# Twelve-tile down projections by single column groups, and a new order for the last down pairs, in a two-layer encoder on one core

## The chip, the core and the metric

The kernel runs on one core of a Trainium2 chip. Such a core has a matrix engine (PE, "TensorE"; its weight loads are shown apart as PEld), a vector engine (DVE), a scalar engine (ACT), GpSimd (POOL), and a sync engine (SP), which here issues the DMAs. Each engine works through its own instructions in the order in which they stand, and waits for the others by semaphores. The metric is the device time of one launch in microseconds (us); less is better. Before the change it was 2042.35 us (median of 3 runs, 2038.47 to 2043.43).

## What is computed

An encoder trunk of two layers over 256 tokens of 2048 features, all in float32: layer 0 mixes tokens by attention, layer 1 by a gated linear recurrence, and each is followed by the same feed-forward part:

```python
D_MODEL = 2048; SEQ = 256; DEPTH = 2
D_FF = -(-8 * D_MODEL // (3 * 256)) * 256        # 5632

def swiglu(h, w_gate, w_up, w_down):
    return (jax.nn.silu(h @ w_gate) * (h @ w_up)) @ w_down

def reference(x, ...):
    for i in range(DEPTH):
        h = rms_norm(x, norm_mix[i])
        mix = attention_mixer(...) if i % N_MIXERS == 0 else recurrent_mixer(...)
        x = x + mix
        x = x + swiglu(rms_norm(x, norm_ffn[i]), w_gate[i], w_up[i], w_down[i])
    return x
```

The change lies in the feed-forward part alone.

## The kernel before

**Numbers in two parts.** A float32 value is held as a high part `hi` (a cast to the matmul's format) and a low part `lo` (the value less `hi`). A product of two tiles is three matmuls: high by high, high by low, low by high. Weights come from memory as blocks `raw` of 512 KB: two tiles of 128 input features, each by 512 output columns (`load_half`, L109). ACT casts a block to `hi` (L122), DVE subtracts to get `lo` (L123). There are five buffers of each of `raw`, `hi` and `lo`, so the cast of a block waits until PE has finished the block five before it. Token tiles are the stationary side of a matmul, weights the moving one, and results gather in accumulators `acc` of 128 tokens by 512 columns. There are four of these (`ps_a`); four more (`pm`) hold other sums.

**The feed-forward part** (`ffn`, L760). The 5632 hidden features are 44 tiles, worked through in three parts of 12, 16 and 16 (`PARTS`). In each part, units of four hidden tiles are made from all 16 tiles of the normalized input (`unit`, L761): one column group of the gate weights and one of the up weights. Then silu, scalings, and a turn from token rows to feature rows (`turned`, L444: two DVE transposes `tb`, then sixteen small ACT copies `tf`), after which ACT writes each hidden tile's high part (`act`, L775) and DVE its low part (L776). When the units of a part are done, `down` (L493) multiplies the part's hidden tiles by its share of the down weights and adds the result to the residual `x_tok`. The output has four column groups of 512.

**Pairs and seven products.** `project_pair` (L276) takes two column groups together (gate and up, or two groups of the down weights) and two halves of the tokens, so it fills all four accumulators. It goes through pairs of input tiles in steps. An ordinary step reads two weight blocks, one for each column group, and makes four products from each. Two steps of each call are made in another way: seven products on sums of blocks instead of eight products. For these, `seven_forms` (L245) makes sums of two weight blocks on DVE (`wx`, L252 to L255), their high part on ACT (`wxh`, L259) and low part on DVE (`wxl`, L260), and `x_forms` (L264) sums of the token tiles. Five of the seven results go through separate sums in `pm`, which `merge` (L317) combines on DVE; `down` then adds them to the residual (L500), apart from the accumulators' own adds (L509). `SEVEN` gives the two steps that are so made, by the number of steps, and `USUAL_STEPS` and `FIRST_STEPS` the order of the steps. A down of 12 tiles has six steps a call, 0, 2, 1, 4, 3, 5, of which 1 and 3 are of seven products.

**One column group at a time.** `output` (L476) and `project_tokens` (L223), which serve the attention's and the recurrence's output projections, take one column group after the other with two accumulators each, all in plain products.

**What sets the order.** PE's order is the order of the code. The other engines' orders, SP's DMA queue among them, are set at build time by a scheduler that goes by the order in which the code asks for things and by its own reckoning of times; on the chip nothing overtakes. `half` (L162) hands out the weight blocks in the order of a list, `order`, and `ffn_order` (L137) builds the feed-forward part of that list, so the steps' order must be the same there and in `project_pair`. The last down of the first layer also feeds the next normalization: `norm.add` (L410) squares a finished column group (`nj`), turns it, and writes the operands `xg` (L404, L405) of the recurrent layer. The last down of the second layer sends each finished group to memory.

## Time and profile before

| | |
|---|---|
| median of 3 runs | 2042.35 us |
| the profiled execution, its device time | 2042.2 us |
| its span, first to last instruction | 2040.4 us |
| mean granted PE clock | 0.990 |
| PE, DVE, ACT busy | 98%, 84%, 65% of the span |
| memory read | 382.13 MB |

The page gives shares of the whole span. In its groups of instructions, a line such as "L282 PE MATMUL acc<-hi,act" names the source line, the engine, the operation and the tiles: out of a weight block's high part and a hidden tile into an accumulator. The view of waits gives, for an engine, the line that waited, the line it waited for, the time in all, how often, and the longest. The windows give busy times and the granted clock for stretches of the span. The view in order of time has a start, a duration and, in brackets, the idle time before an instruction and what ended it. Successive matmuls overlap, so their pace is read from their starts.

### The profile page before, as it was taken

Reading aid. Unit: us, or ns where it says so; the run is one execution under the profiler, and the core shown is the slowest. Engines: PE = TensorE matmul, PEld = TensorE weight load, DVE = VectorE, ACT = ScalarE, POOL = GpSimd, SP = SyncE. Lnnn points to the kernel's source line nnn. Section 1 sums busy time; section 2 is a strip of 40 time slices with the busy share of each in tenths; the row PEclk is TensorE's granted clock in tenths of the full one; section 3 lists DMA queues with packets and bytes.
Section 4 is the critical chain, followed back from the end, with each engine's and each line's share of the span. In section 5 each row is a group of like instructions: output and inputs, shape, how many; then the busy total and the mean of one; then the engine's idle time right before and its main releaser. Section 6 shows DMA issues by size and latency. Waiting matters only on the chain.

```text
span 2040.4 us, 27933 instructions
## 1 busy us (share of the span) xinstructions
PE 1999.7 (98%) x9920; PEld 1691.3 (83%) x9920; DVE 1721.6 (84%) x2447; ACT 1336.3 (65%) x2070; POOL 166.6 (8%) x213
## 2 busy tenths in 40 slices
PE   9999999989999999999899999999989999999999
PEld 8898888867888888888799998888768888888887
DVE  7998789877888878889868877889787889878987
ACT  7665767654667546676689987767535766457663
POOL 1563000000000000000133330000000000000000
PEclk9999999989999999999899999999999999999999
DMA  8444565555556665555646555555545566555664
GB/s 318 156 135 146 184 209 194 186 172 189 186 184 198 208 213 186 186 190 193 200 157 197 180 167 186 186 196 196 177 168 180 188 197 225 190 193 186 204 218 145
DMA packets 109004, 386.06 MB, mean 189 GB/s; under 512 B 12224, under 2 KB 12992, under 8 KB 108736
## 3 DMA queue, kind: packets, MB, share of 16 engines
q1 hardware_dynamic: 108720, 384.26, 56.9%
q8 instruction: 78, 1.28, 0.2%
q14 instruction: 62, 0.51, 0.1%
q10 hardware_dynamic: 144, 0.02, 0.0%
HBM read 382.13 MB, written 2.10 MB: 188 GB/s over the span
## 4 chain that ended last, share of the span: by engine, by line
PE 69%; DVE 17%; DMA 6%; issue 5%; ACT 3%; SPq 0%; POOL 0%; DVEq 0%; ACTq 0%
PE acc L282 38%; PE acc L235 8%; DVE lo L123 7%; PE pm L282 5%; PE acc L213 5%; DMA raw<-in_w_up_dram 4%; PE acc L328 3%; PE acc L327 3%; PE acc L329 3%; ACT tf L456 1%; DMA raw<-in_w_down_dram 1%; ACT hi L122 1%; PE pm L328 1%; PE pm L329 1%; PE pm L327 1%
## 5 line engine op out<-in xcount | busy, mean ns | idle before, releaser
L122 ACT CAST hi<-raw 128x1024 fp32r<-128x1024 f32 (+1 forms) x708 | 730.5, 1047 | 510.9 <-PE acc L282 384.7
L123 DVE TENSOR_TENSOR lo<-raw,hi 128x1024 fp32r<-128x1024 f32 (+1 forms) x708 | 855.0, 1226 | 133.4 <-ACT hi L122 129.6
L282 PE MATMUL acc<-hi,xg 128*128 128x512 f32 x2200 | 698.2, 390 | 9.8 <-DVE x_tok L509 6.0
L282 PEld LDWEIGHTS acc<-hi,xg 128*128 128x128 f32 x2200 | 413.4, 188 | 103.2 <-issue 7.8
L282 PE MATMUL acc<-lo,xg 128*128 128x512 f32 x1100 | 428.6, 390 | 0.0
L282 PE MATMUL acc<-hi,act 128*128 128x512 f32 x1072 | 349.7, 399 | 14.9 <-ACT act L775 7.5
L282 PEld LDWEIGHTS acc<-hi,act 128*128 128x128 f32 x1072 | 205.5, 192 | 65.9 <-ACT act L775 8.3
L282 PEld LDWEIGHTS acc<-lo,xg 128*128 128x128 f32 x1100 | 206.8, 188 | 42.4
L282 PE MATMUL acc<-lo,act 128*128 128x512 f32 x536 | 212.1, 396 | 0.0
L456 ACT COPY tf<-tb 32x256 f32<-32x256 f32 x448 | 181.2, 404 | 8.4 <-DVE xg L405 1.2
L235 PE MATMUL acc<-hi,act 128*128 128x512 f32 x512 | 159.8, 390 | 0.0
L327 PE MATMUL acc<-xg,hi 128*128 128x256 f32 x512 | 146.8, 287 | 3.5 <-ACT xg L404 3.4
L252 DVE TENSOR_TENSOR wx<-raw,raw 128x512 f32<-128x512 f32 x68 | 47.1, 692 | 120.0 <-DMA raw<-in_w_up_dram 89.3
L328 PE MATMUL acc<-xg,hi 128*128 128x256 f32 x512 | 146.5, 286 | 0.8 <-DVE xg L405 0.7
L329 PE MATMUL acc<-xg,lo 128*128 128x256 f32 x512 | 145.9, 285 | 0.0
L260 DVE TENSOR_TENSOR wxl<-wx,wxh 128x1536 fp32r<-128x1536 f32 x68 | 119.2, 1753 | 15.1 <-ACT wxh L259 14.8
L259 ACT CAST wxh<-wx 128x1536 fp32r<-128x1536 f32 x68 | 100.6, 1479 | 44.2 <-DVE wx L255 40.3
L213 PE MATMUL acc<-xg,hi 128*128 128x512 f32 x384 | 126.1, 396 | 0.1
L282 PEld LDWEIGHTS acc<-lo,act 128*128 128x128 f32 x536 | 103.1, 192 | 21.2
L235 PEld LDWEIGHTS acc<-hi,act 128*128 128x128 f32 x512 | 96.1, 188 | 19.6
L327 PEld LDWEIGHTS acc<-xg,hi 128*128 128x128 f32 x512 | 99.7, 195 | 3.9 <-ACT xg L404 3.9
L328 PEld LDWEIGHTS acc<-xg,hi 128*128 128x128 f32 x512 | 99.6, 195 | 1.3 <-DVE xg L405 1.3
(239 smaller groups left out, 2846.3 us busy)
## 6 DMA issues: line engine op xcount, KB each, us to landing
raw<-in_w_gate_dram SPq DMA_DIRECT2D x176, 512.0 KB, 4.4
raw<-in_w_up_dram SPq DMA_DIRECT2D x176, 512.0 KB, 4.2
raw<-in_w_down_dram SPq DMA_DIRECT2D x176, 512.0 KB, 4.3
raw<-in_w_in_dram SPq DMA_DIRECT2D x64, 512.0 KB, 4.4
raw<-in_w_qv_dram SPq DMA_DIRECT2D x40, 512.0 KB, 4.3
raw<-in_w_o_dram SPq DMA_DIRECT2D x32, 512.0 KB, 3.5
raw<-in_w_out_dram SPq DMA_DIRECT2D x32, 512.0 KB, 3.8
graw<-in_w_gates_dram SPq DMA_DIRECT2D x32, 256.0 KB, 3.5
```

The lines of the kernel that those rows point to most:

```text
L122: newest["cast"] = act.copy(hi[:, sl, :], raw[:, sl, :])
L123: dve.tensor_tensor(lo[:, sl, :], raw[:, sl, :], hi[:, sl, :].bitcast(F32), ALU.subtract)
L213: pe.matmul(o, w, x, start=(k == 0 and not part), stop=(k == total - 1 and not part))
L235: pe.matmul(accs[a], x, wt[:, k, :], start=(k0 + k == 0 and n == 0), stop=(end and k == 1 and n == 2))
L252: dve.tensor_tensor(x[:, 0, :], r2[:, 0, :], r1[:, 0, :], ALU.add)
L259: act.copy(xh, x)
L260: dve.tensor_tensor(xl, x, xh[:].bitcast(F32), ALU.subtract)
L282: pe.matmul(acc, a, b, start=id(acc) not in begun, stop=last and i == 2)
L327: pe.matmul(o, hi, x[:, :S], start=start, stop=False)
L328: pe.matmul(o, hi, x[:, S:], start=False, stop=False)
L329: pe.matmul(o, lo, x[:, :S], start=False, stop=stop)
L456: act.copy(o, y)
```

## The change

Downs of 12 tiles no longer use seven-product steps. They go through `output`: four column groups, one after the other, each through steps 0 to 5 in order with two accumulators, and their residual adds are those of `output`. No token sums are made for that part. Downs of 16 tiles stay as they were, apart from the last part's: there each pair of column groups runs its steps together up to and with the second seven-product step (step 5), and then steps 6 and 7 for the first column group and after that for the second. The second pair of the last part also takes step 3 before step 2. `project_pair` now hands each column group's accumulators to a function `done` as soon as they are finished. The list of weight blocks follows.

```diff
-SEVEN = {6: (1, 3), 8: (2, 5)}
-USUAL_STEPS = {6: (0, 2, 1, 4, 3, 5), 8: (0, 1, 2, 3, 4, 5, 6, 7)}
+SEVEN = (2, 5)
+USUAL_STEPS = (0, 1, 2, 3, 4, 5, 6, 7)
 FIRST_STEPS = (0, 1, 3, 4, 2, 6, 5, 7)
+LAST_STEPS = (0, 1, 3, 2, 4, 5, 6, 7)
...
+    def pair_plan(steps, apart):
+        m = 1 + steps.index(SEVEN[-1]) if apart else len(steps)
+        return [(n, (0, 1)) for n in steps[:m]] + [(n, (j,)) for j in range(2) for n in steps[m:]]
+
+    def unit_steps(first):
+        return FIRST_STEPS if first else USUAL_STEPS, False
+
+    def down_steps(p, second):
+        last = p == len(PARTS) - 1
+        return LAST_STEPS if second and last else USUAL_STEPS, last
...
             down = wide(f"w_down{l}_{p}")
+            if n != KT:
+                seq += down
+                continue
             for c in range(0, len(down), n):
-                for k in pair_steps(n // 2):
-                    seq += [down[c + k], down[c + n // 2 + k]]
+                for k, cols in pair_plan(*down_steps(p, c > 0)):
+                    seq += [down[c + n // 2 * j + k] for j in cols]
...
-    def project_pair(xs, forms, middle, first=False):
+    def project_pair(xs, forms, order, middle, done):
...
-        steps = pair_steps(len(xs) // 2, first)
-        seven = [n for n in steps if n in forms]
-        for n in steps:
+        steps = pair_plan(*order)
+        seven = [n for n in order[0] if n in forms]
+        for n, cols in steps:
...
-                for j in range(2):
+                for j in cols:
                     half()
                     hi, lo = (flat(t) for t in newest["tiles"])
+                    end = n == order[0][-1]
                     for a in range(2):
                         for k in range(2):
-                            product(banks[j][a], tokens(2 * n + k, a), (hi[:, k, :], lo[:, k, :]), n == steps[-1] and k == 1)
-        return banks
+                            product(banks[j][a], tokens(2 * n + k, a), (hi[:, k, :], lo[:, k, :]), end and k == 1)
+                    if end:
+                        done(j, banks[j])
...
-            banks = project_pair(xs, forms, middle)
-            for j in range(2):
+            def done(j, accs):
                 for a in range(2):
...
-                        dve.tensor_tensor(y, y, banks[j][a][:, sl], ALU.add)
+                        dve.tensor_tensor(y, y, accs[a][:, sl], ALU.add)
...
+            project_pair(xs, forms, down_steps(p, c > 0), middle, done)
...
-            for i, n in enumerate(seven):
-                if first <= 2 * n < len(hid):
+            for i, n in enumerate(SEVEN):
+                if forms is not None and first <= 2 * n < len(hid):
                     forms[n] = x_forms(hid[2 * n], hid[2 * n + 1], f"hf{i}")

         for p, n in enumerate(PARTS):
-            hid, forms = [], {}
+            hid, forms = [], {} if n == KT else None
...
-            down(hid, forms, nxt if last else None, last and nxt is None)
+            if n == KT:
+                down(hid, forms, p, nxt if last else None, last and nxt is None)
+            else:
+                output(hid)
```

In `unit`, the adds, silu and scalings that stood after `project_pair` move into a `done` of its own, for each column group as it ends.

How the order of instructions moves on the engines is shown at three places. First DVE, at the end of the third unit of the first layer's twelve-tile part: from the adds of the up accumulators (`fu<-acc`) to the transposes. Before:

```order
L123 TENSOR_TENSOR lo_4424<-raw_4422,hi_4423 128x1024
L769 TENSOR_TENSOR fu_4246<-acc_4011,fu_4246 128x512
L769 TENSOR_TENSOR fu_4246<-acc_4012,fu_4246 128x512
L260 TENSOR_TENSOR wxl_4448<-wx_4446,wxh_4447 128x1536
L770 SCALAR_TENSOR_TENSOR fu_4246<-fu_4246,nr_3271,fg_4245 128x512 x2
L123 TENSOR_TENSOR lo_4442<-raw_4440,hi_4441 128x1024
L123 TENSOR_TENSOR lo_4451<-raw_4449,hi_4450 128x1024
L448 STREAM_TRANSPOSE tb_4332<-fu_4246 128x512 x2
```

After:

```order
L124 TENSOR_TENSOR lo_4402<-raw_4400,hi_4401 128x1024
L786 TENSOR_TENSOR fu_4226<-acc_3991,fu_4226 128x512
L786 TENSOR_TENSOR fu_4226<-acc_3992,fu_4226 128x512
L787 SCALAR_TENSOR_TENSOR fu_4226<-fu_4226,nr_3271,fg_4225 128x512 x2
L124 TENSOR_TENSOR lo_4420<-raw_4418,hi_4419 128x1024
L462 STREAM_TRANSPOSE tb_4312<-fu_4226 128x512 x2
```

The block sums' low part and one of two weight rows ahead of the transposes are gone.

Second ACT, a little later at the same place: the sixteen copies and the casts that write the hidden tiles' high parts (`act`). Before:

```order
L456 COPY tf_4333<-tb_4332 32x2x128 x16
L122 CAST hi_4523<-raw_4522 128x1024
L122 CAST hi_4532<-raw_4531 128x1024
L122 CAST hi_4576<-raw_4575 128x1024
L775 CAST act_4352<-tf_4333 128x256
```

After:

```order
L470 COPY tf_4313<-tb_4312 32x2x128 x16
L123 CAST hi_4459<-raw_4458 128x1024
L123 CAST hi_4477<-raw_4476 128x1024
L795 CAST act_4332<-tf_4313 128x256
L795 CAST act_4335<-tf_4313 128x256
```

Two weight casts stand between the copies and the hidden tiles, where there were three. The two belong to the first two blocks of the second column group.

Third DVE again, where that down ends and the next unit begins: the residual adds that free the last accumulators. Before:

```order
L123 TENSOR_TENSOR lo_4926<-raw_4924,hi_4925 128x1024
L254 TENSOR_TENSOR wx_4948<-raw_4951,raw_4942 128x512
L500 TENSOR_TENSOR x_tok<-x_tok,fg_4815 128x512
L500 TENSOR_TENSOR x_tok<-x_tok,fu_4816 128x512
L509 TENSOR_TENSOR x_tok<-x_tok,acc_4617 128x512
L123 TENSOR_TENSOR lo_4944<-raw_4942,hi_4943 128x1024
L255 TENSOR_TENSOR wx_4948<-wx_4948,raw_4942 128x512
L509 TENSOR_TENSOR x_tok<-x_tok,acc_4616 128x512
L509 TENSOR_TENSOR x_tok<-x_tok,acc_4618 128x512
```

After:

```order
L264 TENSOR_TENSOR wx_4874<-raw_4877,raw_4868 128x512
L265 TENSOR_TENSOR raw_4877<-raw_4877 128x512
L124 TENSOR_TENSOR lo_4834<-raw_4832,hi_4833 128x1024
L266 TENSOR_TENSOR wx_4874<-raw_4877,raw_4868 128x512
L267 TENSOR_TENSOR wx_4874<-wx_4874,raw_4868 128x512
L124 TENSOR_TENSOR lo_4852<-raw_4850,hi_4851 128x1024
L498 TENSOR_TENSOR x_tok<-x_tok,acc_4680 128x512
L498 TENSOR_TENSOR x_tok<-x_tok,acc_4681 128x512
```

The merged sums' adds are gone. All four block-sum operations of the next unit's first seven-product step stand ahead of the last two residual adds.

More of the change, by code (lines that the diff above doesn't have):

```diff
@@ L132, in wide @@
         return [(src[c, i], HALF) for c in range(src.shape[0]) for i in range(src.shape[1])]
-    def pair_steps(n, first=False):
-        return FIRST_STEPS if first else USUAL_STEPS[n]
+    def pair_plan(steps, apart):
[6 more added lines that the diff above has]
+        return LAST_STEPS if second and last else USUAL_STEPS, last
     def ffn_order(l):
@@ L141, in ffn_order @@
             for _ in range(n // FOUR):
-                for k in pair_steps(KT // 2, i == 0):
-                    seq += [u[i + k] for u in units]
+                for k, cols in pair_plan(*unit_steps(i == 0)):
+                    seq += [units[j][i + k] for j in cols]
                 i += KT // 2
             down = wide(f"w_down{l}_{p}")
+            if n != KT:
+                seq += down
+                continue
             for c in range(0, len(down), n):
-                for k in pair_steps(n // 2):
-                    seq += [down[c + k], down[c + n // 2 + k]]
+                for k, cols in pair_plan(*down_steps(p, c > 0)):
+                    seq += [down[c + n // 2 * j + k] for j in cols]
         return seq
@@ L414, in add @@
                 self.operand(f, True)
-            for n in SEVEN[KT // 2] if self.seven else ():
+            for n in SEVEN if self.seven else ():
                 if FOUR * c <= 2 * n < FOUR * c + FOUR:
@@ L490, in output, with down @@
             norm.finish()
-    def down(xs, forms, norm=None, end=False):
+    def down(xs, forms, p, norm=None, end=False):
         for c in (0, 2):
@@ L760, in ffn, with unit, done @@
     def ffn(norm, nxt):
-        def unit(hid, forms, seven, first):
+        def unit(hid, forms, first):
             got = []
-            banks = project_pair(norm.xs, norm.forms, lambda *banks: got.extend(merge(*banks)), first)
-            g, u = got
-            for a, acc in enumerate(banks[0]):
-                dve.tensor_tensor(g[:, a, :], acc, g[:, a, :], ALU.add)
-                table_act(g[:, a, :], g[:, a, :], AF.Silu, scale=norm.rt[:, a : a + 1])
-            for a, acc in enumerate(banks[1]):
-                dve.tensor_tensor(u[:, a, :], acc, u[:, a, :], ALU.add)
-                dve.scalar_tensor_tensor(u[:, a, :], u[:, a, :], norm.rt[:, a : a + 1], g[:, a, :], ALU.mult, ALU.mult)
+            def done(j, accs):
+                g, u = got
+                for a, acc in enumerate(accs):
+                    if j == 0:
+                        dve.tensor_tensor(g[:, a, :], acc, g[:, a, :], ALU.add)
+                        table_act(g[:, a, :], g[:, a, :], AF.Silu, scale=norm.rt[:, a : a + 1])
+                    else:
+                        dve.tensor_tensor(u[:, a, :], acc, u[:, a, :], ALU.add)
+                        dve.scalar_tensor_tensor(u[:, a, :], u[:, a, :], norm.rt[:, a : a + 1], g[:, a, :], ALU.mult, ALU.mult)
+            project_pair(norm.xs, norm.forms, unit_steps(first), lambda *banks: got.extend(merge(*banks)), done)
+            u = got[1]
             first = len(hid)
@@ L777, in unit @@
                 hid.append(h)
-            for i, n in enumerate(seven):
-                if first <= 2 * n < len(hid):
+            for i, n in enumerate(SEVEN):
+                if forms is not None and first <= 2 * n < len(hid):
                     forms[n] = x_forms(hid[2 * n], hid[2 * n + 1], f"hf{i}")
         for p, n in enumerate(PARTS):
-            hid, forms = [], {}
+            hid, forms = [], {} if n == KT else None
             for i in range(n // FOUR):
-                unit(hid, forms, SEVEN[n // 2], p == i == 0)
+                unit(hid, forms, p == i == 0)
             last = p == len(PARTS) - 1
@@ L788, in ffn @@
                 ln_exp_tables()
-            down(hid, forms, nxt if last else None, last and nxt is None)
+            if n == KT:
+                down(hid, forms, p, nxt if last else None, last and nxt is None)
+            else:
+                output(hid)
     nr = Norm("norm_mix", KT)
```

## The prediction

> **What bounds the kernel now.** I read the page first, then who waits for whom on TensorE (PE), then the windows with the granted clock, and last the order in time round both twelve-tile down projections.

> ```profile
> span 2040.4 us, 27933 instructions
> PE 1999.7 (98%) x9920; PEld 1691.3 (83%) x9920; DVE 1721.6 (84%) x2447; ACT 1336.3 (65%) x2070; POOL 166.6 (8%) x213
> ...
> PE acc L282 <- DVE x_tok L509: 11.1, 7, 2.4
> PE acc L282 <- ACT act L775: 7.5, 2, 3.8
> PE acc L282 <- DVE fg L766: 4.5, 10, 0.9
> PE acc L327 <- ACT xg L404: 3.4, 1, 3.4
> ...
> PE pm L282 <- DVE wxl L260: 1.4, 1, 1.4
> ```

> PE sets the time; all it lost is in such waits and in slow stretches after them. The waits name the places: residual adds that free an accumulator (L509) and hidden tiles that are late (L775) are 18.6 of them. The next rows are windows (us, each engine's busy time and count, granted clock, DMA share, GB/s): both down projections with their edges, then three stretches inside the first.

> ```profile
> core 0: us, PE busy (x) PEld busy (x) DVE busy (x) ACT busy (x) POOL busy (x), PEclk, DMA share, GB/s
> 394.90:476.70 81.80, 71.82 (x290) 56.30 (x289) 68.25 (x83) 42.02 (x54) 0.00 (x0) 0.94 0.52 170
> 1445.00:1529.00 84.00, 73.72 (x291) 57.64 (x289) 68.30 (x83) 41.49 (x54) 0.00 (x0) 0.91 0.49 164
> ...
> 411.60:422.60 11.00, 6.80 (x17) 4.80 (x17) 6.51 (x8) 6.87 (x11) 0.00 (x0) 0.69 0.43 153
> 436.00:443.00 7.00, 4.68 (x14) 3.13 (x13) 6.66 (x10) 2.43 (x3) 0.00 (x0) 0.76 0.44 137
> 471.00:478.00 7.00, 3.82 (x16) 2.54 (x16) 7.00 (x10) 2.60 (x3) 0.00 (x0) 1.00 0.37 107
> ```

> Now PE in order of time: start, duration, instruction, and in brackets the idle time before it and what ended that.

> ```profile
> 394.94 0.39 PE L282 MATMUL acc<-hi,xg 128*128 128x512 f32 x1
> ...
> 406.58 0.39 PE L282 MATMUL acc<-hi,act 128*128 128x512 f32 x1
> ...
> 411.34 0.39 PE L282 MATMUL acc<-wxh,act 128*128 128x512 f32 x1
> 415.49 0.80 PE L282 MATMUL acc<-hi,act 128*128 128x512 f32 x1 [3.76 <-ACT act L775]
> ...
> 438.59 0.50 PE L282 MATMUL acc<-hi,act 128*128 128x512 f32 x1 [2.32 <-DVE x_tok L509]
> ...
> 470.38 0.39 PE L282 MATMUL acc<-hi,xg 128*128 128x512 f32 x1
> ...
> 474.30 0.50 PE L282 MATMUL acc<-hi,xg 128*128 128x512 f32 x1 [2.40 <-DVE x_tok L509]
> ...
> 476.73 0.47 PE L282 MATMUL acc<-hi,xg 128*128 128x512 f32 x1 [0.78 <-DVE x_tok L509]
> ...
> 1445.08 0.39 PE L282 MATMUL acc<-hi,xg 128*128 128x512 f32 x1
> ...
> 1529.20 0.77 PE L282 MATMUL acc<-hi,xg 128*128 128x512 f32 x1 [0.44 <-DVE x_tok L509]
> ```

> Matmuls overlap, so a duration of 0.39 is not their price. The 21 matmuls of a seven-product step start between 406.58 and 411.34: 4.76 / 21 = **0.2267 us each**; a product of three is 0.68, a weight block of four products 2.72. From 394.94 (the unit's last matmul) to 476.73 (the 13th of the next unit) PE issues 1 + 276 + 12 = 289. At full pace that is 65.5; it took 81.79, so 16.3 are lost: the three waits, the slow stretches, and some 0.7 at the unit's end, where the fg adds behind block sums free the first accumulators late. In the second layer (1445.08 to 1529.20) it took 84.12: 18.6 lost. These 34.9 are the prize.

> **The change, part by part.**

> *Extra matmuls.* A twelve-tile down has 92 products now (two pairs of column groups, each four steps of eight products and two of seven) and 96 after. Four products of three, two layers: 24 x 0.2267 = **+5.4**. Nothing hides them.

> *The first wait: hidden tiles of the last unit.* DVE and ACT in time:

> ```profile
> 397.73 1.28 DVE L769 TENSOR_TENSOR fu<-acc,fu 128x512 f32<-128x512 f32 x2
> 398.93 1.75 DVE L260 TENSOR_TENSOR wxl<-wx,wxh 128x1536 fp32r<-128x1536 f32 x1
> 400.59 1.41 DVE L770 SCALAR_TENSOR_TENSOR fu<-fu,nr,fg 128x512 f32<-128x512 f32 x2
> 401.92 2.36 DVE L123 TENSOR_TENSOR lo<-raw,hi 128x1024 fp32r<-128x1024 f32 x2
> 404.19 1.30 DVE L448 STREAM_TRANSPOSE tb<-fu 128x512 f32<-128x512 f32 x2
> ...
> 405.52 6.65 ACT L456 COPY tf<-tb 32x256 f32<-32x256 f32 x16
> 412.19 2.94 ACT L122 CAST hi<-raw 128x1024 fp32r<-128x1024 f32 x3
> 415.04 1.32 ACT L775 CAST act<-tf 128x256 fp32r<-128x256 f32 x4
> ...
> 416.68 1.43 DVE L776 TENSOR_TENSOR act<-tf,act 128x256 fp32r<-128x256 f32 x4
> ```

> Let T be the unit's end on PE, 394.94 + 0.23 = 395.2. The transposes end at T+10.3, the copies at T+17.0, and PE goes on at T+20.3 although it got there by T+16.4. After the change this chain loses the block sums: behind the two fu adds stand the two scalings, one weight row and the transposes, so about 0.2 + 1.28 + 1.41 + 1.18 + 1.30 = T+5.4. Sixteen copies: T+12.0. Two weight casts instead of three, 2 x 0.98: T+14.0; first tile's cast: T+14.3. But PE is there sooner too: it needs tile 8 after four weight blocks, 4 x 2.72 = T+10.9, since the order is now by column group. So the wait stays, about 3.4. The tile's low half stands behind the low halves of two weight blocks on DVE: about T+15.7, with the third matmul due at T+14.8: 0.9 more. Bounds: 0, if the chain outruns this, to 9.4, if operands still come at T+20.3. The queues' new order, not the old time, speaks for 4.3. Behind the casts ACT also holds weight casts, but those are for blocks that PE reaches later.

> Then the slow stretch. The window 411.60:422.60 has a mean clock of 0.69: (1 - 0.69) x 11.0 = 3.4 lost. I take 3.4 again. First wait after: 3.4 + 0.9 + 3.4 = **7.7 per layer**.

> [...]

> *The second and third wait: accumulators.* There are four accumulators. A pair of column groups takes all four, so the next pair (438.59) and the next unit (474.30, 476.73) wait until DVE has added them into x_tok, and DVE has merges and block sums in between:

> ```profile
> 466.42 0.69 DVE L252 TENSOR_TENSOR wx<-raw,raw 128x512 f32<-128x512 f32 x1 [0.25 <-DMA raw<-in_w_up_dram]
> ...
> 472.36 0.68 DVE L500 TENSOR_TENSOR x_tok<-x_tok,fg 128x512 f32<-128x512 f32 x1
> ...
> 473.56 0.68 DVE L509 TENSOR_TENSOR x_tok<-x_tok,acc 128x512 f32<-128x512 f32 x1
> ```

> After the change a column group takes two, and the other two have a whole group, 6 x 2.72 = 16.3, to be added: hidden. At the next unit, its first block uses the accumulators of the group before the last; the last group's are needed 2.72 and 4.08 after the down's end. Before those adds DVE has the next unit's four block-sum operations and two weight rows. The first of them now runs at 466.42, 4.0 ahead of the next unit's start at 470.38; four at 0.60 a step and two at 1.14 end 0.7 after it, and the adds at 1.3 and 1.9. That is in time by 1.4. If the cover goes, PE waits one for one, up to today's 2.40 + 0.78 here. I take 0.

> Both spans then need 301 x 0.2267 = 68.2 plus 7.7 = 75.9: **-5.9** against 81.79, **-8.2** against 84.12; the extra matmuls are inside.

> *The last part's pairs.* The products are the same. In each pair the last two steps run one column group, then the other; the first group's accumulators are finished 5.44 before the pair's end, not 2.72, and their adds and normalization start earlier. In the second pair step 2 (seven products) follows step 3. Where the first layer's normalization lies over block sums, PE waits 1.4 for wxl; with step 2 later I take it as gone: **-1.4**, bounds -1.4 to +3 (the same wait, doubled, at step 2). Weight DMAs on SP move with the steps, and one output DMA of the second layer is put ahead of one more weight DMA; that block is used only in the fourth step, so PE's 16.3 of earlier products hide it. Exposed, it would cost a landing, under 5.

> After the first layer PE waits for the next normalization and for gate operands:

> ```profile
> 996.21 0.58 PE L327 MATMUL acc<-xg,hi 128*128 128x256 f32 x1 [3.45 <-ACT xg L404]
> 997.46 0.58 PE L328 MATMUL acc<-xg,hi 128*128 128x256 f32 x1 [0.66 <-DVE xg L405]
> ...
> 1014.53 0.35 PE L327 MATMUL pm<-xs,ghi 128*128 128x256 f32 x1 [1.44 <-DVE xs L364]
> ```

> The third column group's adds may start 2.7 earlier, but one more weight cast and weight row stand ahead of the same xg rows, and gate DMAs move ahead of weights. I take 0, between -4.1 (3.45 + 0.66 gone) and +3.4 (another slow stretch). At the kernel's end the last accumulator is the same one: 0.

> **Sum.** -5.9 - 8.2 - 1.4 = -15.5 on a span of 2040.4: 2024.9. The profiled execution took 2042.2, so 1.8 lie around its span, and the median of the runs is 2042.35: **2027 us**.

> **Rivals.**
> 1. *The first wait goes.* The chain is 6 us shorter, and ACT need only run a little earlier than I count. For: DVE is freed. Against: sixteen copies (6.65) alone fill most of T+10.9. 2027 - 2 x 7.7 = 2012.
> 2. *The next unit still waits.* The last group's adds stay behind block sums that wait for a DMA (0.25 at 466.42). Today's price is 2.40 + 0.78, with half of a 3.4 slow stretch about 4.9 per layer: 2037. Against: 1.4 of slack.
> 3. *No slow stretch* follows the first wait. For: not every wait has one, 2.40 at 474.30 had none (1.00 in 471:478). Against: 2.32 had one, and 3.76 one of 3.4. Without it in both layers: 2027 - 2 x 3.4 = 2020. [...]
> 4. *Slower: every column group waits for its accumulators.* If DVE falls behind by more than the 16.3 of a group, each of the four group ends per layer costs what one costs now: (2.32 + 2.40 + 0.78) / 2 and a slow stretch of (1 - 0.76) x 7.0 = 1.7 make 4.5. That is 8 x 4.5 = 36 put on 2027: 2063. For: DVE is 84% busy. Against: without block sums a group needs six weight rows (7.4) and two adds (1.4) of those 16.3.
> 5. *The wait only moves*: operands still at T+20.3, so 9.4 + 3.4 per layer: 2027 + 2 x 5.1 = 2037.

> **Numbers.** Forecast 0.68, rivals in order 0.07, 0.08, 0.08, 0.04, 0.05. The likeliest one's own range is 2020 to 2034, two slow stretches either way. For 8 in 10 I take 2015 to 2037: it leaves out rival 4, most of rival 1, and the forecast's tails. What can be told from no change is 0.3%, 6.1 us, so faster means below 2036.2: the forecast, rivals 1 and 3 and half of 2, some 0.87. Rival 5 and the rest of 2 make 0.08 for no change; rival 4 and a tail 0.05.

> **What would show it.** In the new profile: 24 more matmuls; no wait on a residual add of the down (x_tok) in either down or at the unit behind it; a wait of 3 to 4 for the act cast, some 11 us into each down, with a half-clock stretch behind it; no wait on wxl in the first layer's last part. Each span from unit's end to the 13th matmul of the next unit should be 73 to 79. Accumulator waits at column group ends, a first wait over 6 or none, or a new wait of more than 3 where the recurrent layer starts would each prove a step wrong.

## The result and the profile after

The changed kernel takes **2028.24 us** (median of 4 runs, 2026.79 to 2030.66) against 2041.95 for the kernel before (4 runs, the three named above and one more): a ratio of 0.9936, 95% interval 0.9919 to 0.9954. It is faster by 13.7 us. The forecast was 2027, with a range of 2015 to 2037. The profiled execution took 2027.33; its span is 14.9 shorter than the one before (2040.4).

The page of the changed kernel: the span, the engines' busy time, and then PE's first waits (what waited, for whom, us in all, times, longest).

```profile
span 2025.5 us, 27859 instructions
PE 1994.5 (98%) x9944; PEld 1690.0 (83%) x9944; DVE 1665.6 (82%) x2347; ACT 1318.7 (65%) x2054; POOL 167.4 (8%) x213
...
PE acc L294 <- DVE fg L783: 5.9, 9, 1.6
PE acc L247 <- ACT act L795: 5.3, 2, 2.7
PE pm L294 <- DVE wxl L272: 2.3, 1, 2.3
PE acc L341 <- ACT xg L418: 2.3, 1, 2.3
...
PE acc L342 <- DVE xg L419: 1.8, 1, 1.8
PE acc L247 <- DVE act L796: 1.5, 2, 0.7
...
PE acc L294 <- DVE x_tok L522: 0.6, 1, 0.6
```

PE has the 24 matmuls more, DVE 100 instructions and 56 us less. The 11.1 of waits on residual adds (x_tok) are down to 0.6, and that one stands in the last part. The wait for the hidden tiles (act) is there, once in each layer. The wait for wxl, forecast to go, grew from 1.4 to 2.3.

The two spans (from the start of the unit's last matmul to the start of the 13th of the next unit) as windows of the changed kernel, and then the stretch behind the first wait; the columns are those of the windows before.

```profile
394.77:468.61 73.84, 70.43 (x303) 57.51 (x301) 42.78 (x48) 35.21 (x46) 0.00 (x0) 0.98 0.56 177
1439.57:1513.39 73.82, 70.41 (x302) 57.50 (x301) 42.75 (x48) 35.21 (x46) 0.00 (x0) 0.98 0.55 178
408.70:415.10 6.40, 5.66 (x16) 4.18 (x17) 3.57 (x6) 2.64 (x5) 0.00 (x0) 0.73 0.68 229
```

DVE's work in a span fell from 68.3 to 42.8. PE's 301 matmuls ask 301 x 0.2267 = 68.24, so 5.6 are lost in each span, where 16.3 and 18.6 were. PE in order of time shows where they are in the first layer:

```profile
394.77 0.39 PE L294 MATMUL acc<-hi,xg 128*128 128x512 f32 x1
394.99 0.39 PE L247 MATMUL acc<-hi,act 128*128 128x512 f32 x1
...
405.65 0.39 PE L247 MATMUL acc<-hi,act 128*128 128x512 f32 x1
408.70 0.50 PE L247 MATMUL acc<-hi,act 128*128 128x512 f32 x1 [2.67 <-ACT act L795]
...
410.18 0.74 PE L247 MATMUL acc<-hi,act 128*128 128x512 f32 x2 [0.74 <-DVE act L796]
...
465.89 0.39 PE L294 MATMUL acc<-hi,xg 128*128 128x512 f32 x1
...
468.38 0.61 PE L294 MATMUL acc<-hi,xg 128*128 128x512 f32 x2
```

There is one wait of 2.67, one of 0.74 right behind it, a slowed stretch (a clock of 0.73 over 6.4: 1.7 lost), some 0.5 of starts and ends, and then nothing up to the next unit and in it.

### The profile page after: what moved, and what is told of

It is laid out like the page before. It is cut to its first block, busy times and chain, and to the rows that moved or that the text cites. A ratio compares the mean times of both kernels' runs of the same rounds, so it can differ in the third digit from the quotient of the medians.

```text
span 2025.5 us, 27859 instructions
## 1 busy us (share of the span) xinstructions
PE 1994.5 (98%) x9944; PEld 1690.0 (83%) x9944; DVE 1665.6 (82%) x2347; ACT 1318.7 (65%) x2054; POOL 167.4 (8%) x213
## 3 DMA queue, kind: packets, MB, share of 16 engines
q8 instruction: 78, 1.28, 0.3%
## 4 chain that ended last, share of the span: by engine, by line
PE 74%; DVE 14%; issue 4%; DMA 4%; ACT 3%; POOL 0%; SPq 0%; DVEq 0%; ACTq 0%; POOLq 0%
PE acc L294 38%; PE acc L247 14%; DVE lo L124 6%; PE pm L294 6%; PE acc L225 4%; DMA raw<-in_w_up_dram 3%; PE acc L342 3%; PE acc L341 3%; PE acc L343 3%; ACT tf L470 1%; PE pm L342 1%; PE pm L343 1%; PE pm L341 1%; ACT hi L123 1%; DVE tb L462 1%
## 5 line engine op out<-in xcount | busy, mean ns | idle before, releaser
L123 ACT CAST hi<-raw 128x1024 fp32r<-128x1024 f32 (+1 forms) x708 | 729.9, 1046 | 512.3 <-PE acc L294 331.3
L247 PE MATMUL acc<-hi,act 128*128 128x512 f32 x896 | 281.5, 393 | 6.8 <-ACT act L795 5.3
L294 PE MATMUL acc<-hi,act 128*128 128x512 f32 x800 | 253.7, 390 | 1.8 <-DVE fg L783 1.2
L247 PEld LDWEIGHTS acc<-hi,act 128*128 128x128 f32 x896 | 169.6, 189 | 43.5 <-ACT act L795 6.2
L294 PEld LDWEIGHTS acc<-hi,act 128*128 128x128 f32 x800 | 150.2, 188 | 36.2 <-issue 3.2
L247 PE MATMUL acc<-lo,act 128*128 128x512 f32 x448 | 175.6, 392 | 0.0
L294 PE MATMUL acc<-lo,act 128*128 128x512 f32 x400 | 155.7, 389 | 0.0
L264 DVE TENSOR_TENSOR wx<-raw,raw 128x512 f32<-128x512 f32 x60 | 41.5, 692 | 126.3 <-DMA raw<-in_w_up_dram 102.5
L272 DVE TENSOR_TENSOR wxl<-wx,wxh 128x1536 fp32r<-128x1536 f32 x60 | 105.0, 1751 | 11.2 <-ACT wxh L271 11.2
L271 ACT CAST wxh<-wx 128x1536 fp32r<-128x1536 f32 x60 | 88.7, 1478 | 38.4 <-DVE wx L267 35.5
```

The lines of the kernel that those rows point to most:

```text
L123: newest["cast"] = act.copy(hi[:, sl, :], raw[:, sl, :])
L247: pe.matmul(accs[a], x, wt[:, k, :], start=(k0 + k == 0 and n == 0), stop=(end and k == 1 and n == 2))
L264: dve.tensor_tensor(x[:, 0, :], r2[:, 0, :], r1[:, 0, :], ALU.add)
L271: act.copy(xh, x)
L272: dve.tensor_tensor(xl, x, xh[:].bitcast(F32), ALU.subtract)
L294: pe.matmul(acc, a, b, start=id(acc) not in begun, stop=last and i == 2)
```

## The experiments

Twelve kernels ran, each timed against the kernel before on the same chip (its medians there: 2039.4 to 2040.7). "Lost" is the length of each span, measured as above, less its matmuls at 0.2267.

| kernel | twelve-tile down | last part | median us | ratio, 95% interval | lost in the two spans |
|---|---|---|---|---|---|
| before | pairs, two seven-product steps each | old | 2041.95 | 1 | 16.3, 18.6 |
| the change | single groups, none | new | 2028.24 | 0.9936 (0.9919-0.9954) | 5.6, 5.6 |
| e1 | single groups, none | old | 2026.03 | 0.9932 (0.9919-0.9944) | 6.2, 5.6 |
| e2 | as before | new | 2042.76 | 1.001 (1.0-1.002) | 15.8, 16.7 |
| e3 | pairs, none | new | 2017.07 | 0.9885 (0.987-0.99) | 0, 0.1 |
| e5 | pairs with split ends, none | new | 2015.45 | 0.988 (0.9866-0.9893) | 0, 0 |
| e12 | first two groups as a pair, then single, none | new | 2015.72 | 0.988 (0.9861-0.9899) | 0, 0 |
| e4 | pairs with split ends, two at places 3 and 4 | new | 2028.12 | 0.9937 (0.9926-0.9949) | 9.6, 10.5 |
| e8 | pairs with split ends, two at places 2 and 3 | new | 2033.44 | 0.9965 (0.9954-0.9976) | 11.9, 10.8 |
| e7 | pairs with split ends, one at place 3 | new | 2015.26 | 0.9874 (0.9861-0.9887) | 1.9, 2.1 |
| e6 | as e5 | old | 2014.6 | 0.9875 (0.9861-0.9889) | 0, 0 |
| e9 | as e5, two in the second pair alone | old | 2009.8 | 0.9854 (0.9838-0.9869) | 0.7, 0.7 |
| e10 | as e9, and one in the first pair at place 4 | old | 2018.02 | 0.9893 (0.9878-0.9907) | 4.5, 3.8 |
| e11 | as e5 | split ends, old step order | 2014.78 | 0.9874 (0.9859-0.989) | 0, 0 |

"Split ends" means that a pair's last two steps run for one column group and then for the other.

### The two parts of the change apart: e1 and e2

e1 undoes the last part's new order, and e2 the twelve-tile change.

```diff
     def down_steps(p, second):
-        last = p == len(PARTS) - 1
-        return LAST_STEPS if second and last else USUAL_STEPS, last
+        return USUAL_STEPS, False
```

> The changed kernel with the last part's pairs in their old order, so that the twelve-tile change stands alone. Theory A (all of the gain comes from the two twelve-tile downs): the two spans are as in the changed kernel, 301 matmuls and about 5.6 lost in each, so 8.0 + 10.3 = 18.3 below the kernel before in them; the wxl wait of the first layer's last part goes back to some 1.5 and stands at its second seven-product step. Time 2024 to 2029, which is the changed kernel's 2028 or a little below. Theory B (the last part's new order carries part of it, by its earlier adds and normalization): the recurrent layer's start loses some 4 more again, time 2031 or above.

For e2 and all that follow, twelve-tile downs go through `down` again, with steps of their own. Here they are as in the kernel before; `APART_12` is the number of steps that both groups take together, 0 for all.

```diff
+SEVEN_12 = (1, 3)
+STEPS_12 = (0, 2, 1, 4, 3, 5)
+APART_12 = 0
     def pair_plan(steps, apart):
-        m = 1 + steps.index(SEVEN[-1]) if apart else len(steps)
+        m = apart or len(steps)
...
     def down_steps(p, second):
+        if PARTS[p] != KT:
+            return STEPS_12, APART_12
         last = p == len(PARTS) - 1
-        return LAST_STEPS if second and last else USUAL_STEPS, last
+        return LAST_STEPS if second and last else USUAL_STEPS, 6 * last
...
-            if n == KT:
-                down(hid, forms, p, nxt if last else None, last and nxt is None)
-            else:
-                output(hid)
+            down(hid, forms, p, nxt if last else None, last and nxt is None)
```

> The kernel before with the last part's new order alone; the twelve-tile downs run in pairs with block sums as before. Theory A: within 3 of the kernel before, 2039 to 2045, with the wxl wait at the first seven-product step of the second pair (about 2.5) in place of 1.4 at its later place. Theory B: 4 or more below the kernel before, since the normalization starts earlier.

Theory A held in both: the gain is the twelve-tile downs'. e1 took 2026.03 and e2 2042.76. In e1 the wait for wxl is back at 1.4; in e2 it is 2.3, as in the change, and the old accumulator waits are all there (first e1's waits of PE, then e2's):

```profile
PE acc L246 <- ACT act L794: 5.3, 2, 2.7
...
PE pm L293 <- DVE wxl L271: 1.4, 1, 1.4
```

```profile
PE acc L296 <- DVE x_tok L524: 11.7, 8, 2.3
...
PE pm L296 <- DVE wxl L274: 2.3, 1, 2.3
```

Whether the last part's order costs anything in all is at the edge of what these runs tell: e2's interval reaches from 0 to 0.2% slower.

### Which half of the twelve-tile change gains: e3, e5, e12

The change does two things there: it leaves the block sums out, and it takes column groups singly. e3 does the first without the second.

```diff
-SEVEN_12 = (1, 3)
-STEPS_12 = (0, 2, 1, 4, 3, 5)
+SEVEN_12 = ()
+STEPS_12 = (0, 1, 2, 3, 4, 5)
```

> The changed kernel, but its twelve-tile downs run in pairs of column groups again, all four accumulators at once; block sums stay left out, so the 24 matmuls stay. Theory A (what made PE wait for accumulators is the merges and block sums that stood ahead of the adds on DVE): no more than 3 of waits per layer on x_tok adds, and hidden tiles are needed only at 8 weight blocks, 21.8 after the unit's end, while they come at 13.7: no wait for the act cast. The spans lose at most 4 each; time 2022 to 2028. Theory B (a pair that holds all four accumulators waits whatever stands in DVE's queue): the old waits of 2.3 at the second pair and 2.4 + 0.8 at the next unit stay with a slow stretch, so 8 or more lost in each span, time 2032 or above.

e5 sets `APART_12 = 4` besides.

> As the plain pairs, without block sums, but each pair ends with its last two steps for one column group, then for the other, so two of the four accumulators are finished 5.4 before the other two and have that long to be added. Theory A (late operands and late accumulators are all that the two downs lose): neither wait is left, tiles 8 to 11 are first needed 21.8 after the unit's end; each span loses under 1.5 and there is no slow stretch; time 2028 - 2 x 4.5 = 2019, 2016 to 2022. Theory B (the loss only moves, to the next unit's start or to the operands of the second pair): 4 or more lost per span, time 2025 or above.

e12 runs the first two groups as a pair and the last two singly:

```diff
+APART_12 = -1
...
+        m = max(apart, 0) if apart else len(steps)
...
+            return STEPS_12, APART_12 if second else 0
```

> The changed kernel, but the first two column groups of each twelve-tile down run as a pair; the last two stay one after the other. Block sums stay out, the last part stays as in the changed kernel. Theory A (all that the column order costs is the first wait: a single group asks for the hidden tile 8 at 10.9 after the unit's end, a pair at 21.8, and its operand comes at 13.7): no wait for the act cast and no slow stretch, both spans at full pace (under 1 lost in each), 2 x 5.6 = 11.1 below the changed kernel's 2028.2: 2015 to 2019. Rival (the column order as such costs, at the change from one group to the next): 2022 or above.

Theory A held in all three. e3 went 5 below the range that was expected for it, e5 half a microsecond; e12 fell inside. The spans as windows, e3 and then e12:

```profile
395.29:463.51 68.22, 68.22 (x302) 56.51 (x301) 41.37 (x48) 35.12 (x46) 0.00 (x0) 1.00 0.59 187
1433.25:1501.58 68.33, 68.33 (x303) 56.34 (x301) 40.66 (x47) 34.54 (x46) 0.00 (x0) 1.00 0.60 186
```

```profile
395.37:463.60 68.23, 68.23 (x303) 56.50 (x302) 41.60 (x48) 35.12 (x46) 0.00 (x0) 1.00 0.60 188
1436.08:1504.30 68.22, 68.22 (x302) 56.49 (x301) 42.56 (x48) 35.13 (x47) 0.00 (x0) 1.00 0.61 192
```

PE is busy for the whole of each window, at full clock: 68.2 for 301 matmuls is the pace itself. So leaving the block sums out gains some 24 (e3 against the kernel before), and **taking the first two groups singly gives 11 of them back**. What it gives back is the first wait alone. ACT of e3 shows that the hidden tiles come no sooner:

```profile
400.21 6.63 ACT L472 COPY tf<-tb 32x256 f32<-32x256 f32 x16 [0.68 <-DVE tb L464]
406.86 2.00 ACT L126 CAST hi<-raw 128x1024 fp32r<-128x1024 f32 x2
408.77 1.32 ACT L797 CAST act<-tf 128x256 fp32r<-128x256 f32 x4
```

The unit ends in e3 at 395.29 + 0.23 = 395.52, so the first cast ends about 408.77 + 0.4, 13.7 later: as in the changed kernel. A pair asks for it 21.8 after the unit's end, a single group 10.9 after. And a pair that takes all four accumulators does not wait for them by itself: in e3 neither span has such a wait.

### Can the block sums stay? e4, e8, e7

These take e5 and put seven-product steps back. e4 has `SEVEN_12 = (1, 3)` with steps 0, 2, 1, 3, 4, 5.

> Block sums kept in the twelve-tile downs (the 24 matmuls go again), and each pair ends with its last two steps one column group after the other, so that two accumulators are free 5.4 earlier. Theory V (VectorE is the bound there: 68.25 of its work between the unit's end and the 13th matmul of the next unit in the kernel before, where TensorE at full pace needs 65.5): early accumulators cannot help, at least 2.7 and, with slow stretches, some 8 are lost in each span; time 2026 or above. Theory E (what cost time was only that the accumulators came free at the very end of a pair): the x_tok waits go and the 5.4 come on top, time 2012 to 2016.

e8 has `SEVEN_12 = (1, 2)`, and e7 `SEVEN_12 = (2,)`, both with steps 0 to 5 in order.

> As the run with one seven-product step, but with two, the second and the third of the six, early in each pair, so that the merge is done long before the pair ends; all 24 matmuls go: 5.4. Theory V: VectorE has as much to do as in the kernel before, some 68 per span against 65.5 of TensorE, so it falls behind somewhere, at the seven-product steps (wxl) or at the accumulators; at least 2.7 lost per span, time 2015 to 2030. Rival (it was the place of the merge late in the pair, not the amount of work): no loss, time 2010 to 2013.

> As the pairs with endings apart, but one of the six steps of each twelve-tile pair is a seven-product step again (the third), so 12 of the 24 matmuls go: 2.7. Theory V: a pair now asks some 27 of VectorE for its 32 of TensorE, so it keeps up, no wait on x_tok adds over 1; time 2015.5 - 2.7 = 2012.8, 2011 to 2015. Rival (any merge ahead of the adds brings the accumulator waits back): two waits of about 2.3 per layer with slow stretches, time 2020 or above.

By its time e4 is as theory V has it (2026 or above). e8 is slower than theory V's range of 2015 to 2030. e7 just misses the range of 2011 to 2015, is far from its rival's 2020, and so is no faster than e5 although it has 12 matmuls less. The profiles do not bear the theory out as it was put, by VectorE's total: neither e4 nor e8 has a wait on x_tok in the spans, nearly all that they lose stands in one place, and the longest wait there is for ACT. PE of e4, then ACT and PE of e8:

```profile
418.95 0.80 PE L296 MATMUL pm<-wxh,hf 128*128 128x512 f32 x1 [2.75 <-ACT wxh L273]
421.18 0.80 PE L296 MATMUL pm<-wxl,hf 128*128 128x512 f32 x1 [1.44 <-DVE wxl L274]
```

```profile
407.44 6.61 ACT L472 COPY tf<-tb 32x256 f32<-32x256 f32 x16
414.07 1.47 ACT L273 CAST wxh<-wx 128x1536 fp32r<-128x1536 f32 x1
```

```profile
415.60 0.79 PE L296 MATMUL pm<-wxh,hf 128*128 128x512 f32 x1 [6.57 <-ACT wxh L273]
417.39 0.79 PE L296 MATMUL pm<-wxl,hf 128*128 128x512 f32 x1 [1.00 <-DVE wxl L274]
```

In e8 the high part of the block sums (wxh) stands behind the sixteen copies of the unit's end on ACT, and PE waits 6.57 for it. In e4 wxh stands behind the copies, four weight casts and the hidden tiles' casts; the same step waits twice 0.8 for its weights, and 3.4 go in a slowed stretch. In both kernels and both layers that is the *first* pair, some 30 us behind the unit's end; the second pair, with as many sums, waits 0.4 for wxl and no more. In e7 one of a down's two seven-product steps stands there too, and its merge runs ahead of the hidden tiles' low halves on DVE. With a wait of 1.31 for these (act, on DVE) in each layer, the spans lose 1.9 and 2.1, more than the 1.36 that each saves in matmuls. So a new theory, B: the sums hurt where they meet the burst of scalings, transposes, copies and casts at a unit's end.

### Theory B tried: e9, e10, and a faster kernel

e9 keeps the sums in the second pair alone, e10 has one step of them in the first pair as well (`FIRST_SEVEN_12 = (3,)`). Both have the last part in its old order, for which e6 is the measure.

> Pairs without block sums and with endings apart in the twelve-tile downs, as before, and the last part in its old order. Theory A (the last part's new order costs about 2, as the two runs with and without it say: 2028.2 and 2026.0, 2042.8 and 2040.7): 2013 to 2014. Rival (those differences are spread between runs): 2015.5, as with the new order.

```diff
+SEVEN_12 = (1, 3)
+FIRST_12 = (0, 1, 2, 3, 4, 5)
+FIRST_SEVEN_12 = ()
+STEPS_12 = (0, 2, 1, 3, 4, 5)
...
+            return STEPS_12 if second else FIRST_12, APART_12
...
-            project_pair(xs, forms, down_steps(p, c > 0), middle, done)
+            some = forms if c or PARTS[p] == KT else {n: forms[n] for n in FIRST_SEVEN_12}
+            project_pair(xs, some, down_steps(p, c > 0), middle, done)
```

> The pairs with endings apart and the last part in its old order (2014.6), but the second pair of each twelve-tile down has two seven-product steps again, so 12 of the 24 matmuls go: 2.7. Theory B (block sums hurt only in the first pair, where they meet the unit's last burst of scalings, transposes, copies and hidden-tile casts on VectorE and ScalarE; the amount of work in a whole span does not matter, since two runs with all block sums lost nothing after the first 15 us of it): no wait in the second pair or at the next unit; 2014.6 - 2.7 = 2011.9, 2010 to 2013. Theory V (VectorE's total): half of the added work is back, a wait on an x_tok add of 1 or more at the next unit, time 2014 or above.

> As the run with seven-product steps in the second pair alone, but the first pair has one as well, as its fourth step (16.3 after the unit's end, the last hidden tiles' casts are at 13.7 to 16.5): 18 of the 24 matmuls go, 4.1. Theory B with the burst over by then: 2014.6 - 4.1 = 2010.5. Theory B with the burst not over (its block sums and the low halves of the hidden tiles stand in one queue): a wait of 2 or more for wxl or wxh in the first pair or for act at the fifth step, with a slow stretch, 3 to 7 per layer: 2016 to 2024.

e6 took 2014.6: half a microsecond over what was expected with the old order, one below e5, and so not told apart from it. e9 took **2009.8**, the lowest median of all, as theory B has it and a little under the 2010 to 2013 that were expected. Its two spans as windows:

```profile
394.26:461.84 67.58, 67.16 (x296) 55.31 (x295) 53.75 (x65) 36.90 (x49) 0.00 (x0) 1.00 0.62 196
1431.56:1499.14 67.58, 67.16 (x296) 55.32 (x295) 53.83 (x65) 36.96 (x49) 0.00 (x0) 1.00 0.59 191
```

DVE has 53.8 of work there, 11 more than in the change, and the clock stays at 1.00; the one wait is 0.4 for wxl. Against pairs without sums (68.23) each span is 0.65 shorter, 1.3 in all. The rest of the 4.8 between e6 and e9 lies outside the spans, in waits that differ by 1 or 2 from build to build; what moved it was not found out.

What e9 does not part is place and amount, since it also has half of the sums. The loss goes up with DVE's work in a span: none at 41 to 42 (e3, e5), 0.7 at 54 (e9), 2 at 59 (e7), some 4 at 62 (e10), 10 to 12 at 67 (e4, e8). No run has all of the sums away from a unit's end. What speaks for place is the inside of e4 and e8: as many sums stand in the second pair as in the first, and it waits 0.4.

e10 took 2018.02, as the second theory has it, but not by the wait that it named. There is no wait for wxh, wxl or act in the first pair; the second pair waits 1.0 and 0.5 for wxl. But the merge of the first pair, some five later behind the unit's end than e7's and spread among low halves on DVE, put off the residual adds, and the accumulator wait was back although the endings were split (one in each layer; DVE and PE, first layer):

```profile
424.50 0.69 DVE L525 TENSOR_TENSOR x_tok<-x_tok,acc 128x512 f32<-128x512 f32 x1
425.10 0.69 DVE L339 TENSOR_TENSOR fg<-pm,fg 128x512 f32<-128x512 f32 x1
...
430.97 0.69 DVE L525 TENSOR_TENSOR x_tok<-x_tok,acc 128x512 f32<-128x512 f32 x1
```

```profile
431.72 0.50 PE L297 MATMUL acc<-hi,act 128*128 128x512 f32 x1 [2.69 <-DVE x_tok L525]
```

### The wait for wxl in the last part: e11

e11 is e5 with the old step order in the last part's second pair, the endings still split: `LAST_STEPS = (0, 1, 2, 3, 4, 5, 6, 7)`.

> As the pairs with endings apart and the last part's new endings (2015.45), but the second pair of the last part has its seven-product steps at the old places (third and sixth) while the last two steps stay one column group after the other. Theory S (the 2.3 wait for wxl comes from step 2 being run as the fourth, when the first pair's normalization fills VectorE): the wait goes or falls under 1.5, time 2013 to 2015. Theory N (it comes from the earlier normalization that the split endings bring): the wait stays at 2 or more, at step 2 or 5, time 2015 to 2018.

The single wait of 2.3 became two small ones, at step 2 and at step 5:

```profile
943.40 0.50 PE L296 MATMUL pm<-wxl,hf 128*128 128x512 f32 x1 [0.94 <-DVE wxl L274]
...
959.67 0.50 PE L296 MATMUL pm<-wxl,hf 128*128 128x512 f32 x1 [0.33 <-DVE wxl L274]
```

Theory S held in the profile. DVE of the changed kernel shows what step 2 meets as the fourth step:

```profile
948.89 2.38 DVE L468 COPY tf<-tb 32x256 f32<-32x256 f32 x8
951.30 0.69 DVE L267 TENSOR_TENSOR wx<-wx,raw 128x512 f32<-128x512 f32 x1
...
954.18 1.67 DVE L419 SCALAR_TENSOR_TENSOR xg<-tf,pk,xg 128x256 fp32r<-128x256 f32 x4
955.77 1.75 DVE L272 TENSOR_TENSOR wxl<-wx,wxh 128x1536 fp32r<-128x1536 f32 x1
```

The last block sum (L267) stands behind eight small copies of the normalization, and wxl behind its xg rows, while PE needs wxl at 955.1. In the time, 2014.78 against 2015.45, the two orders cannot be told apart.

## Why the prediction was right, and where it was not

**The extra matmuls**, +5.4: as forecast, 24 of them, not hidden.

**The first wait** was where it was put, with the two waits and the slow stretch that were forecast, and mis-sized: 5.6 lost in each layer, where 7.7 were counted. The wait itself, 2.67, is below the 3 to 4 that the prediction gave as its sign. DVE and ACT of the changed kernel:

```profile
394.71 1.28 DVE L786 TENSOR_TENSOR fu<-acc,fu 128x512 f32<-128x512 f32 x2
...
398.36 1.30 DVE L462 STREAM_TRANSPOSE tb<-fu 128x512 f32<-128x512 f32 x2
...
399.70 6.63 ACT L470 COPY tf<-tb 32x256 f32<-32x256 f32 x16 [0.69 <-DVE tb L462]
...
408.25 1.32 ACT L795 CAST act<-tf 128x256 fp32r<-128x256 f32 x4
```

T, the unit's end, is 394.99 here. The transposes end at T+4.7, not T+5.4, since the first of the fu adds starts 0.3 before the unit's end; copies and casts keep their forecast lengths, and the first tile is there at T+13.7, not T+14.3. PE arrived at T+10.9, as forecast. The larger part of the miss is the slow stretch: 1.7 where 3.4 was taken from a stretch that had followed a longer wait (3.76). That stretch had (1 - 0.69) x 11.0 / 0.5 = 6.8 at half clock, twice what came here (the last section has the working). None of the five rivals came; e3, e5 and e12 show what rival 1 (no first wait) was worth.

**The accumulator waits** went to nothing, in both downs and at the unit behind, as forecast, and DVE's last two adds come early enough:

```profile
465.98 1.28 DVE L498 TENSOR_TENSOR x_tok<-x_tok,acc 128x512 f32<-128x512 f32 x2
```

The first is done about 466.66 and wanted at 468.61. The reason given was half of it. The prediction named the pair that takes all four accumulators and the merges and block sums on DVE together. The runs show that the first alone brings no such wait (e3), and that sums and a merge can bring it back even where two accumulators are freed early (e10). That e4 and e8 have none does not clear the sums: PE had lost some 9 or more in the first pair by then, time in which DVE could catch up. So the cure that the change chose for the accumulators, single groups, was not needed once the sums were out, and it is what made the first wait bind.

**The spans** were forecast at 75.9 and measured 73.8: -8.0 and -10.3 in place of -5.9 and -8.2, 4.1 more gain than counted.

**The last part** was forecast at -1.4 by a wait for wxl that would go. This step failed, and in its sign: with step 2 later, the wait moved from step 5 to step 2 and became 2.3, which lies inside the bounds but on their other side. In the prediction's words step 2 "follows step 3" and so would have more time; in fact (e11) that place put its sums into the normalization.

**The recurrent layer's start**, 0: the waits for xg were 3.45 + 0.66 and are now 2.3 + 1.8, so it held. **Elsewhere**, not in the prediction: the small waits of units for the fg adds rose from 4.5 to 5.9 in all. The span fell by 14.9, the two spans by 18.2, so 3.3 were lost outside, where -1.4 was forecast; in the list of waits wxl has 0.9 more, the fg adds 1.4 and x_tok in the last part 0.6, and the rest was not traced. That the forecast came within 1.3 is in part luck, because two misses met: the spans' gain was counted 4.1 too small, and the rest of the kernel 4.7 too fast.

## What to carry to other kernels

When an engine holds up the matrix engine in one stage, ask which work meets which there, and not only how much of it there is: in e4 and e8 the block sums cost some 10 per span, nearly all of it in the first pair, and half as many of them, some 30 us away from the unit's end (e9), cost under 1. A change that does two things (fewer vector operations, another order of columns) should be tried by halves, since one half may pay for the other's loss, here 24 gained and 11 given back. And before operands are asked for earlier by a new loop order, work out when they come: the order by single groups asked for the last tiles 2.8 before they were there.

## What the runs showed of the hardware

The slow stretches behind waits cannot be read off the wait's length, here for waits of 2.3 to 2.7. The wait of 2.67 in the changed kernel is followed by one (that of 2.66 in its second layer too), and PE is at full clock for 2.2 more us, from 408.70 to 410.91, before it comes. The wait of 2.69 in e10 has none (a clock of 1.00 in 426:440 of that run), nor has that of 2.56 in its second layer (the 32 matmuls from 1472.24 to 1479.84 start 0.24 apart). And one and the same wait, for wxl in the last part, stands at 2.3 in eight kernels' lists of waits: behind it e2 (2.26) has a slow stretch, with matmuls 0.43 apart up to 967.30, and so has e5 (2.27); the changed kernel (2.30) has none. Windows round it, of the changed kernel and of e5:

```profile
955.00:965.00 10.00, 7.70 (x35) 6.13 (x34) 9.90 (x12) 4.72 (x5) 0.00 (x0) 1.00 0.50 164
```

```profile
948.00:958.00 10.00, 7.73 (x27) 5.93 (x26) 9.90 (x12) 4.71 (x5) 0.00 (x0) 0.83 0.51 167
```

With 0.73 over 6.4 and 0.83 over 10.0, the time at half clock is (1 - 0.73) x 6.4 / 0.5 = 3.5 and (1 - 0.83) x 10.0 / 0.5 = 3.4: one piece of the same length.

```profile
407.50:410.91 3.41, 1.47 (x5) 0.93 (x6) 3.41 (x6) 3.02 (x6) 0.00 (x0) 1.00 0.33 82
410.91:414.32 3.41, 3.41 (x10) 2.63 (x9) 1.36 (x2) 0.04 (x1) 0.00 (x0) 0.50 0.80 288
953.63:957.04 3.41, 1.64 (x8) 1.02 (x6) 3.41 (x6) 1.76 (x2) 0.00 (x0) 1.00 0.94 318
```

```profile
947.31:950.72 3.41, 1.14 (x6) 0.62 (x4) 3.41 (x7) 1.17 (x2) 0.00 (x0) 1.00 0.96 332
```

```profile
427.04:430.46 3.42, 1.99 (x9) 1.31 (x7) 3.42 (x5) 1.06 (x1) 0.00 (x0) 1.00 0.50 163
```

The first has PE busy for 1.47 of 3.41 (43%), and the piece behind it is at half clock. The third, which holds most of the wait for wxl, has 1.64 (48%), and full clock goes on. In e5 the same wait lies within one piece, 1.14 (33%), and half clock follows (the 0.83 above); in e10 the wait of 2.69 is cut in two, 1.99 (58%) and 2.15 (63%) in the next piece, and nothing follows (1.00 in 426:440). In the traces of the kernel before and of the changed one, the 13 pieces at full clock that were followed by half clock had PE busy for 0 to 43%, and the 1158 others for 48% at least (the third row above, and 1.65 of 3.42 in 473.19:476.61 of the kernel before). PE's ends are modelled, so these shares are rough, and no line is drawn between the two sorts.
